# Operands of four operand sets made one stage early, kept in DRAM and fetched back, with four plain openings left out

## The chip, the cores and the metric

The kernel runs on one core of one Trainium2 chip. The metric is the time of one execution on the device in microseconds (us), lower is better; the profile is one execution taken by the hardware profiler.

## The reference

One encoder layer on 768 tokens (512 of the sample, 256 of the prompt) with 2048 channels, in float32. What matters here:

```python
h = _rms(x, norm_g) * (1 + scl) + shift            # adaLN: shift, scl, gate = silu(c) @ w_ada + b_ada
proj = h @ w_in                                    # 2048 -> 10240 = 80 blocks of 128 features
pool_u, pool_z, q, k, v, attn_z, g_pool, g_attn = split(proj)
pool_y = _pool_mixer(pool_u, pool_w, pool_scale) * silu(pool_z)
attn_y = _neighbourhood_attention(rms(q), rms(k), v, rpb) * silu(attn_z)
merged = sigmoid(g_pool) * (pool_y @ w_pool_up) + sigmoid(g_attn) * (attn_y @ w_attn_up)
return x + gate * (merged @ w_o)
```

## The kernel before

Everything lies with channels on the 128 partitions and the 768 tokens along the free dimension, in two halves of 384. A float32 value is split into two float32r pieces, high and low, and a product is made of three matmuls on them (high by high, weight high by operand low, weight low by operand high).

**Sets.** A set holds the operands of a quarter-size scheme with seven products: for four pairs `j` of channel tiles it has the tiles B11, T1, T2, B21, T3, T4, B22, 28 slots of 384 KB (high and low piece of 128x384). `T1` to `T4` are sums and differences of the raw quarters. The sets follow each other on TensorE: XA and XB (the two halves of the 2048 channels of h, both against all 80 blocks of `w_in`), XR (the mixer's result, against `w_pu`), XY (the attention's result, against `w_au`), MA and MB (the two halves of merged, against `w_o`).

**Jobs.** `pair_job` makes two blocks of 128 outputs out of seven products: 7 x 4 x 3 = 84 matmuls of 128x384. Jobs of one `pair_jobs` list overlap by two products, so that TensorE goes from job to job. `opening` makes the first two blocks of a set without the scheme, from the raw quarters B11, B12, B21, B22 in 96 matmuls (line L458), so that T1 to T4 may be made meanwhile. XB, XR, XY, MA and MB each begin with an opening.

**Order.** The program is written out by hand. `steps` runs TensorE's list; `prepare` keeps the weights' split (L329 on ScalarE, L330 and L353 on VectorE) three products ahead; a clock ticks once in two `j` (six matmuls, 14 ticks in a job), and all other work is put at a tick (`at`, `after`) or in the list `tasks`, which `pump` works off in order when there are slots. `build` puts a set's making into `tasks`: load raw tiles, split them with `Set.put` (a cast on ScalarE, L194, and a subtraction on VectorE, L198), make the differences (`differences`, L218 to L230). There are 45 slots. A set takes 28 of them, and so the next set is mostly made while the last job of the set in front gives its slots back, and in the opening. For XY the raw tiles are the attention's result, gated there with silu of `attn_z` (L1178, L1179).

Other work beside TensorE's: stage A also computes the modulation (`late_mm`); the first part of stage B the pooling mixer (`mix`, with sums on GpSimd, L712); the rest of stage B the attention of 8 head pairs, one every 42 ticks (three jobs) for the first `DENSE` = 5, then one every 56 (four jobs). Partial results go to `part_d` by transfers from GpSimd's queue, in stage B by accumulating ones. SP's queue loads the weights.

Of the kernel before, what the change touches and what calls it, by code (L numbers as in the profile page):

```python
# [16 lines left out]
P = 128  # L17
# [26 lines left out]
SLOTS = 45  # L44
# [7 lines left out]
def encoder_layer(ctx: ExitStack, tc: tile.TileContext, xT, cT, w_ada2, w_ada4, b_ada, norm_g, w_in, pool_w,  # L52
# [14 lines left out]
    heap = {"live": 0, "peak": 0, "spare": 6}  # L67
# [87 lines left out]
    pace = {"kind": "pair", "task": 0, "chore": 0}  # L155
    EVERY = {"plain": 1, "drop": 2, "pair": 3}

    def pump():
        now = clock["now"]
        if tasks and now >= pace["task"] and tasks[0][1]() and room() >= tasks[0][0] + heap["spare"]:  # L160
            pace["task"] = now + EVERY[pace["kind"]]
            tasks.pop(0)[2]()
# [24 lines left out]
    class Set:  # L187
        def __init__(self, name, pairs=PAIRS):
            self.name, self.pairs, self.ops, self.left = name, pairs, {}, 0
# [91 lines left out]

    hurry = {"on": False}
# [62 lines left out]
    def pair_job(stt, f1, f2, done, last=False):  # L345
# [24 lines left out]
        def p1():  # L370
            keep("p1")
            c["o1"], c["o2"] = output("o1"), output("o2")

        def p12():
            dve.tensor_tensor(c["o1"][:, 0, :], c["b"][:, :TH], c["p1"], op=ALU.add)

        def s3():
            keep("u3")
            dve.scalar_tensor_tensor(c["o2"][:, 1, :], c["u3"], -1.0, c["c"][:, :TH], op0=ALU.mult, op1=ALU.subtract)
# [169 lines left out]
    def attention(p, start, pace):  # L549
# [4 lines left out]
        def unit_(u):  # L554
# [110 lines left out]
            def out():  # L665
# [5 lines left out]
                if u == 5:  # L671
                    pool.dma_start(attn_d[p], o)
                    state["attended"] = p
                    free(2)

            stages = [(-6, fetch), (0, scores), (1, biased), (3, exps), (5, vtrans), (6, vsplit), (5, recip), (6, norm),
                      (9, ptrans), (10, psplit), (13, values), (14, out)]
            for d, fn in stages:
# [144 lines left out]
    def fourth(ps):  # L823
# [6 lines left out]
    pair_jobs([pair_job(XA, cut(w_in, a, 0), cut(w_in, b, 0), both(store_part(a), store_part(b)), n == len(jobsA) - 1)  # L830
               for n, (a, b) in enumerate(jobsA)])
# [30 lines left out]
    DENSE = 5  # L862
# [5 lines left out]
    for n, g in enumerate(GR):  # L868
        f = 2 * g
        zz = jobB(Z0 + f, Z0 + f + 1, z_done(f), z_done(f + 1))  # L870
        if n == 0:
            opening(XB, cut(w_in, U0 + f, 1), cut(w_in, U0 + f + 1, 1), u_done(f), u_done(f + 1))
            pair_jobs([zz])
        else:
            pair_jobs([jobB(U0 + f, U0 + f + 1, u_done(f), u_done(f + 1)), zz])
# [16 lines left out]
    pair_jobs([jobB(*j, n == len(jobs) - 2) for n, j in enumerate(jobs[1:])])  # L892


    def sig_load(f):
        state["sig", f] = slot("sig")
        sp.dma_start(flat(state["sig", f]), part_d[G0 + f])

    def sig_take(f):
        t = state["sig", f]  # L900
        act.activation(flat(t), flat(t), AF.Sigmoid)  # L901
        return t

    def pu_done(f):
        def go(i, t):
            sg = sig_take(f)
            dve.tensor_tensor(flat(t), flat(t), flat(sg), op=ALU.mult)
            pool.dma_start(mp_d[f], flat(t))
            free()
            release(t, 3)  # L910
            sig_load(f + 2)
        return go

    def au_done(f):
        def go(i, t):
            sg = sig_take(16 + f)
            dve.tensor_tensor(flat(t), flat(t), flat(sg), op=ALU.mult)  # L917
            free()
            if 16 + f + 2 < 32:
                sig_load(16 + f + 2)  # L920

            def add():
                pool.dma_start(flat(t), mp_d[f], accum_op=ALU.add)
                after(5, out)
# [5 lines left out]
            add()  # L930
# [37 lines left out]
    def eight(stt, w, s, done):  # L968
        opening(stt, cut(w, 0, s), cut(w, 1, s), done(0), done(1))
        pair_jobs([pair_job(stt, cut(w, 2 * i, s), cut(w, 2 * i + 1, s), both(done(2 * i), done(2 * i + 1)), i == 7)  # L970
                   for i in range(1, 8)])

    eight(XR, w_pu, 0, pu_done)
    eight(XY, w_au, 0, au_done)
# [321 lines left out]
```

## Time and profile before

| | |
|---|---|
| median of 3 runs | 2046.11 us (2041.65 to 2046.28) |
| the profiled execution | 2051.03 us, its span from first to last instruction 2049.3 us |
| mean granted TensorE clock | 0.973 of full speed |
| TensorE matmul busy | 1939.6 us, 95% |
| VectorE, ScalarE, GpSimd busy | 1330.4 (65%), 1023.1 (50%), 259.8 us (13%) |
| DMA | 331.92 MB, 162 GB/s over the span |

TensorE is the engine that is nearly always busy; the share tells the mean of stages with different limits, so the stretches where its matmuls come slower than elsewhere have to be looked for one by one. The stages in the trace: XA to about 690 us, XB with the mixer to 900 and with the attention to about 1470, XR to 1630, XY to 1780, MA to 1910, MB to the end.

### The profile page before, as it was taken

What the parts mean: (1) busy time and instruction counts of PE and PEld (TensorE: products, weight loads), DVE (VectorE), ACT (ScalarE), POOL (GpSimd) and SP (SyncE); (2) the same over time, 40 slices, a digit from 0 to 9 for tenths busy, and PEclk for the clock granted to TensorE, in tenths of its full rate; (3) what the DMA queues carried; (4) which work ended last, traced back from release to release, by engine and by line L of the source; (5) the groups of instructions that cost most, each with busy time, mean ns of one, the idle gap of its engine ahead of it and who ended that gap; (6) DMA issues with size and microseconds to landing.
All of it is one profiled execution on the core that took longest, in us unless ns stands there. A gap on an engine that the chain in (4) does not pass through costs nothing. (4 is left out here: it accounts for less than half of the span.)

```text
span 2049.3 us, 31584 instructions
## 1 busy us (share of the span) xinstructions
PE 1939.6 (95%) x11812; PEld 1832.7 (89%) x11812; DVE 1330.4 (65%) x2392; ACT 1023.1 (50%) x2207; POOL 259.8 (13%) x385
## 2 busy tenths in 40 slices
PE   3999999999999989999999999999989979999998
PEld 2889888898999979999998999999979968999997
DVE  5755555555667777866666667667667767776654
ACT  4433333333344444545656566565556555556553
POOL 0000000000000045410000010010100001112111
PEclk9999999999999999999999999999989989999999
DMA  9755555554343425554544344554556556867765
GB/s 355 248 197 188 190 191 191 201 192 157 117 150 138 162 57 143 135 132 106 119 106 122 93 110 122 109 121 123 132 164 216 214 158 180 243 180 191 211 172 144
DMA packets 100361, 331.92 MB, mean 162 GB/s; under 512 B 13168, under 2 KB 18288, under 8 KB 100208
## 3 DMA queue, kind: packets, MB, share of 16 engines
q1 hardware_dynamic: 68256, 217.35, 31.5%
q0 software_dynamic: 30944, 112.48, 23.8%
q8 instruction: 92, 1.51, 0.3%
q14 instruction: 61, 0.50, 0.1%
q10 hardware_dynamic: 1008, 0.09, 0.0%
HBM read 251.22 MB, written 78.64 MB: 161 GB/s over the span
## 5 line engine op out<-in xcount | busy, mean ns | idle before, releaser
L330 DVE TENSOR_TENSOR wlo<-wraw,whi 128x512 fp32r<-128x512 f32 (+1 forms) x357 | 247.2, 693 | 300.7 <-ACT whi L329 294.8
L330 DVE TENSOR_TENSOR wlo<-wsum,whi 128x512 fp32r<-128x512 f32 x420 | 292.7, 697 | 126.6 <-ACT whi L329 124.5
L440 PE MATMUL acc<-xbT,whi 128*128 128x384 f32 x1248 | 338.4, 352 | 10.6 <-ACT u L368 8.4
L329 ACT CAST whi<-wsum 128x512 fp32r<-128x512 f32 x420 | 260.4, 620 | 150.0 <-ACT whi L329 47.2
L440 PE MATMUL acc<-xaT,whi 128*128 128x384 f32 x1216 | 313.5, 338 | 1.1 <-ACT u L368 0.6
L329 ACT CAST whi<-wraw 128x512 fp32r<-128x512 f32 (+1 forms) x357 | 215.8, 605 | 97.4 <-PE acc L440 71.0
L368 ACT COPY u<-acc 128x384 f32<-128x384 f32 x210 | 100.5, 478 | 299.8 <-PE acc L440 299.8
L440 PE MATMUL acc<-xbB,whi 128*128 128x384 f32 x936 | 245.7, 343 | 0.5 <-DVE o L757 0.5
L440 PEld LDWEIGHTS acc<-xbT,whi 128*128 128x128 f32 x1248 | 226.2, 194 | 19.3 <-ACT u L368 10.6
L440 PE MATMUL acc<-xaB,whi 128*128 128x384 f32 x912 | 235.3, 338 | 0.0
L440 PEld LDWEIGHTS acc<-xaT,whi 128*128 128x128 f32 x1216 | 217.5, 188 | 16.2 <-issue 14.4
L440 PE MATMUL acc<-xbT,wlo 128*128 128x384 f32 x624 | 214.8, 344 | 0.0
L440 PE MATMUL acc<-xaT,wlo 128*128 128x384 f32 x608 | 203.7, 335 | 0.0
L440 PEld LDWEIGHTS acc<-xaB,whi 128*128 128x128 f32 x912 | 163.0, 188 | 11.9 <-issue 9.9
L440 PEld LDWEIGHTS acc<-xbB,whi 128*128 128x128 f32 x936 | 165.7, 189 | 6.0 <-issue 1.4
L440 PE MATMUL acc<-xbB,wlo 128*128 128x384 f32 x468 | 157.2, 336 | 0.0
L353 DVE TENSOR_TENSOR wsum<-wraw 128x512 f32<-128x512 f32 x210 | 145.1, 691 | 13.7 <-DMA wraw<-in_w_in_dram 13.6
L440 PE MATMUL acc<-xaB,wlo 128*128 128x384 f32 x456 | 152.8, 335 | 0.0
L353 DVE TENSOR_TENSOR wsum<-wsum,wraw 128x512 f32<-128x512 f32 x210 | 147.7, 703 | 0.2
L440 PEld LDWEIGHTS acc<-xbT,wlo 128*128 128x128 f32 x624 | 121.1, 194 | 0.0
L382 ACT ACTIVATE o<-acc 128x384 f32<-128x384 f32 x105 | 51.6, 492 | 125.3 <-PE acc L440 125.0
L440 PEld LDWEIGHTS acc<-xaT,wlo 128*128 128x128 f32 x608 | 114.1, 188 | 0.0
(251 smaller groups left out, 3435.4 us busy)
## 6 DMA issues: line engine op xcount, KB each, us to landing
wraw<-in_w_in_dram SPq DMA_DIRECT2D x160, 512.0 KB, 4.3
adaw<-in_w_ada_dram SPq DMA_DIRECT2D x96, 512.0 KB, 5.4
part_d<-o POOLq DMA_DIRECT2D x116, 384.0 KB, 2.9
wraw<-in_w_o_dram SPq DMA_DIRECT2D x32, 512.0 KB, 6.2
o<-part_d POOLq DMA_DIRECT2D x38, 384.0 KB, 4.8
sig<-part_d SPq DMA_DIRECT2D x32, 384.0 KB, 6.2
wraw<-in_w_pu_dram SPq DMA_DIRECT2D x16, 512.0 KB, 4.5
wraw<-in_w_au_dram SPq DMA_DIRECT2D x16, 512.0 KB, 5.0
```

The lines of the kernel that those rows point to most:

```text
L329: act.copy(hi[:, :n, :], raw)
L330: dve.tensor_tensor(lo[:, :n, :], raw, hi[:, :n, :].bitcast(F32), op=ALU.subtract)
L353: dve.tensor_tensor(t[:, :n, :], a, b, op=ALU.add)
L368: act.copy(t, c["a"][:, :TH])
L382: act.activation(c["o2"][:, 0, :], c["a"][:, :TH], AF.Copy, scale=-1.0)
L440: pe.matmul(out, w, m, start=s["first"] and j == 0 and k == 0, stop=j == n - 1 and k == 2, skip_group_check=True)
```

## The change

For XB, XR, XY and MB there is no opening: their first two blocks become an ordinary pair job, and their jobs stand in one list with those of the set in front, so that the last job of one set overlaps the first of the next. MA keeps its opening.

`store` makes a set's operands one stage early, out of a second list `back` that `pump` works off beside `tasks` (one entry in three ticks, at most `fly` tiles on their way): raw tiles are loaded, each operand is made with `Set.put` as before, written to DRAM by GpSimd's queue, and its slot is given back four ticks later. `recall` fetches the 28 operands into slots by GpSimd's queue, at most one a tick. XB is made in stage A, XR and XY during the attention, MB during MA. B12 is not made for these sets.

The attention's result is gated in the attention: `attn_z` loaded by SP, silu on ScalarE with a table load before and one after it, a product on VectorE. `DENSE` is 8, so every head pair takes 42 ticks. The sigmoids of the merge gates are taken six ticks after their load. In XB's making the modulation runs on ScalarE, where VectorE did it. 46 slots.

```diff
-SLOTS = 45
+SLOTS = 46
...
+    def store(st, load, ready=lambda j: True, make=None, last=None):
+        got = {}
+        def fetch(j):
+            got["a"], got["b"] = load(j)
+            got["t"] = clock["now"]
+        def save(op, j):
+            t = st.ops.pop((op, j))
+            st.saved[op, j] = d = dram.tile([P, 2, TH], F32R, name=f"{st.name}{op}{j}")
+            pool.dma_start(d, t)
+            def landed():
+                free()
+                heap["flying"] -= 1
+            after(4, landed)
...
+        def pair(j):
+            back.append((2, lambda: ready(j) and free_slot(), lambda: fetch(j)))
+            here = lambda: clock["now"] >= got["t"] + 6
...
+    def recall(st):
+        def load(op, j):
+            t = st.ops[op, j] = slot(f"{st.name}{op}", F32R)
+            pool.dma_start(t, st.saved[op, j])
+        for op in ORDER:
+            for j in range(st.pairs):
+                tasks.append((1, lambda op=op, j=j: (op, j) in st.saved, lambda op=op, j=j: load(op, j), 1))
...
+            def gate_on():
+                act.activation(flat(c["z"]), flat(c["z"]), AF.Silu)
+                act.preload_act_table_set(LNEXP)
...
-    DENSE = 5
+    DENSE = 8
...
-        if n == 0:
-            opening(XB, cut(w_in, U0 + f, 1), cut(w_in, U0 + f + 1, 1), u_done(f), u_done(f + 1))
-            pair_jobs([zz])
...
+    pair_jobs([*line, *eight(XR, w_pu, 0, pu_done), *eight(XY, w_au, 0, au_done)])
+    opening(MA, cut(w_o, 0, 0), cut(w_o, 1, 0), half_done(0), half_done(1))
+    pair_jobs([*eight(MA, w_o, 0, half_done, 1), *eight(MB, w_o, 1, y_done)])
...
-        build(XB, x_pair, lambda j: clock["now"] >= early, x_make, 0, 2)
+        recall(XB)
...
+        store(XR, lambda j: stored(pooled_d, 2 * j))
+        store(XY, lambda j: stored(attn_d, 2 * j), lambda j: state.get("gated", -1) >= 2 * j + 1)
...
+    store(MB, lambda j: stored(merged_d, 8 + 2 * j), lambda j: {8 + 2 * j, 9 + 2 * j} <= state.get("merged", set()))
+    run(16)
+    recall(MB)
```

TensorE's order before, where XR ends and XY begins (L440 are pair jobs, L458 the opening; `xrB`, `xyB` are tiles of the sets):

```order
L440 MATMUL acc<-xrB_15968,whi 128x384 x2
L440 MATMUL acc<-xrB_15968,wlo 128x384
L458 MATMUL acc<-xyB_16287,whi 128x384
L458 MATMUL acc<-xyB_16319,whi 128x384
L458 MATMUL acc<-xyB_16287,whi 128x384
L458 MATMUL acc<-xyB_16319,whi 128x384
L458 MATMUL acc<-xyB_16287,wlo 128x384
```

The same place after the change (L528 are pair jobs):

```order
L528 MATMUL acc<-xrT_16180,whi 128x384 x2
L528 MATMUL acc<-xrT_16180,wlo 128x384
L528 MATMUL acc<-xyB_16327,whi 128x384 x2
L528 MATMUL acc<-xyB_16327,wlo 128x384
L528 MATMUL acc<-xyB_16339,whi 128x384 x2
L528 MATMUL acc<-xyB_16339,wlo 128x384
L528 MATMUL acc<-xyB_16349,whi 128x384 x2
L528 MATMUL acc<-xyB_16349,wlo 128x384
L528 MATMUL acc<-xyB_16363,whi 128x384 x2
L528 MATMUL acc<-xyB_16363,wlo 128x384
L528 MATMUL acc<-xrT_16223,whi 128x384 x2
```

XY's first product now stands between two of XR's last job, where the opening stood behind all of them.

GpSimd's queue before, where MA ends and MB begins (L938 accumulates, L944 and L952 write results):

```order
L938 DMA o_19625<-in_xT_dram 128x768
L938 DMA o_19624<-in_xT_dram 128x768
L944 DMA half_d_258<-o_19625 128x768
L944 DMA half_d_257<-o_19624 128x768
L938 DMA po<-half_d_243 128x768
L938 DMA po<-half_d_244 128x768
```

The same place after the change, up to the last operand of MB (L363 is `recall`'s fetch, L1032 accumulates, L1038 writes):

```order
L363 DMA mbT_20274<-mbT_19215 128x768
L363 DMA mbT_20286<-mbT_19541 128x768
L1032 DMA o_20247<-in_xT_dram 128x768
L363 DMA mbT_20298<-mbT_19870 128x768
L363 DMA mbT_20312<-mbT_20219 128x768
L1032 DMA o_20216<-in_xT_dram 128x768
L363 DMA mbB_20324<-mbB_19052 128x768
L363 DMA mbB_20337<-mbB_19391 128x768
L1038 DMA half_d_258<-o_20247 128x768
L363 DMA mbB_20346<-mbB_19722 128x768
L363 DMA mbB_20358<-mbB_20054 128x768
L1038 DMA half_d_257<-o_20216 128x768
```

Fetches stand between the accumulating transfers and the writes of results, and the last ones stand behind the last of MA's accumulating transfers.

ScalarE's order after the change, in the attention, at a gate (L767, L768 the gate, L200 the cast of `Set.put`, L416 the weights' cast, L675 and L686 the softmax, L455 a copy of a finished sum):

```order
L686 ACTIVATE p<-p,rc 128x192 x2
L200 CAST xrT_10064<-in 128x384
L758 COPY o<-op 64x128 x2
L767 ACT_TABLE_LOAD
L767 ACTIVATE az<-az 128x768
L768 ACT_TABLE_LOAD
L416 CAST whi<-wraw 128x512
L455 COPY u_10111<-acc 128x384
```

The two table loads, the silu and the casts of the stored sets are new between the softmax, the weights' casts and the copies.

## Rows read from the trace of the kernel before

**Rows 1.** The profile page: span; busy time, share and instructions of TensorE.

```profile
span 2049.3 us, 31584 instructions
...
PE 1939.6 (95%) x11812; PEld 1832.7 (89%) x11812; DVE 1330.4 (65%) x2392; ACT 1023.1 (50%) x2207; POOL 259.8 (13%) x385
```

**Rows 2.** Busy time by stretch: start:end, length, engines (x instructions), clock, DMA share, GB/s.

```profile
540.00:690.00 150.00, 150.00 (x868) 150.00 (x867) 104.34 (x176) 65.75 (x127) 10.79 (x20) 1.00 0.39 136
690.00:790.00 100.00, 86.36 (x460) 83.04 (x459) 74.83 (x117) 43.76 (x88) 38.20 (x50) 0.94 0.44 116
790.00:900.00 110.00, 106.86 (x616) 105.29 (x615) 81.84 (x131) 55.78 (x107) 44.80 (x68) 0.99 0.54 138
1038.60:1103.50 64.90, 63.78 (x401) 58.67 (x401) 42.92 (x91) 39.07 (x110) 5.78 (x7) 0.97 0.46 106
...
1485.00:1560.00 75.00, 64.48 (x331) 61.95 (x330) 52.79 (x93) 42.98 (x79) 5.63 (x8) 0.91 0.54 172
1560.00:1620.00 60.00, 58.79 (x339) 58.38 (x338) 46.89 (x78) 33.56 (x61) 4.32 (x8) 1.00 0.61 215
1620.00:1720.00 100.00, 81.87 (x395) 77.06 (x394) 65.36 (x108) 55.44 (x95) 8.93 (x13) 0.86 0.54 170
1720.00:1780.00 60.00, 58.43 (x337) 58.11 (x336) 47.57 (x80) 32.93 (x62) 11.71 (x16) 1.00 0.89 241
1780.00:1835.00 55.00, 48.91 (x270) 47.95 (x269) 38.20 (x68) 31.37 (x64) 8.86 (x13) 0.97 0.70 190
...
1905.00:1955.00 50.00, 47.49 (x271) 46.53 (x270) 32.67 (x59) 29.11 (x59) 9.42 (x13) 1.00 0.67 174
1955.00:2010.00 55.00, 55.00 (x319) 55.00 (x319) 32.91 (x55) 29.47 (x56) 10.80 (x15) 1.00 0.74 188
```

**Rows 3.** TensorE's waits, 1620 to 1720 us: total us, times, longest us.

```profile
PE acc L440 <- ACT p L368: 6.8, 1, 6.8
PE acc L458 <- DVE xyB L198: 4.4, 2, 3.2
```

**Rows 4.** ScalarE in order of time at the same seam: start us, us, instruction.

```profile
1624.30 1.28 ACT L1178 ACT_TABLE_LOAD   x1
...
1626.97 1.28 ACT L901 ACT_TABLE_LOAD   x1
1628.26 0.85 ACT L901 ACTIVATE sig<-sig 128x768 f32<-128x768 f32 x1
```

**Rows 5.** Order of time at the seam of XA and XB.

```profile
738.69 2.07 POOL L712 TENSOR_TENSOR sum<-sum 128x785 f32<-128x785 f32 x1
738.95 2.36 DVE L353 TENSOR_TENSOR wsum<-wsum,wraw 128x512 f32<-128x512 f32 x1
...
746.04 0.50 PEld L440 LDWEIGHTS acc<-xbT,whi 128*128 128x128 f32 x2 [5.25 <-ACT u L368]
```

**Rows 6.** Busy time by stretch, matmuls of the pair jobs (L440) alone, in the attention.

```profile
972.50:1233.50 261.00, 203.19 (x1009) 175.77 (x1008) 0.97 0.47 110
1313.50:1391.50 78.00, 65.23 (x336) 58.82 (x336) 0.98 0.51 118
```

**Rows 7.** TensorE's waits in the attention, 910 to 1460 us: the longest group.

```profile
PE n L503 <- ACT sq L497: 2.1, 5, 0.4
```

**Rows 8.** Groups by line, ScalarE and VectorE: xcount | busy us, mean ns | idle before.

```profile
L194 ACT CAST xyT<-in 128x384 fp32r<-128x384 f32 x16 | 8.2, 512 | 18.8 <-DVE in L223 7.2 <-DVE in L218 6.2 <-DVE in L230 5.4
...
L1178 ACT ACTIVATE in<-in 128x768 f32<-128x768 f32 x8 | 6.5, 841 | 2.9 <-DMA in<-part_d 2.9
...
L198 DVE TENSOR_TENSOR xyT<-in,xyT 128x384 fp32r<-128x384 f32 x16 | 8.7, 552 | 1.2 <-ACT xyT L194 1.2
...
L1179 DVE TENSOR_TENSOR in<-in 128x768 f32<-128x768 f32 x8 | 7.5, 956 | 7.0 <-ACT in L1178 7.0
```

**Rows 9.** Transfers by line: count, KB each, median us from issue to landing.

```profile
part_d<-o POOLq DMA_DIRECT2D x116, 384.0 KB, 2.9
...
o<-part_d POOLq DMA_DIRECT2D x38, 384.0 KB, 4.8
```

More of the change, by code (lines that the diff above doesn't have):

```diff
@@ L280, in build, with put, done, free_slot @@
                 tasks.append((1, lambda: True, lambda j=j, n=n: diff(j, n)))
+    def store(st, load, ready=lambda j: True, make=None, last=None):
[11 more added lines that the diff above has]
+            after(4, landed)
+        def put(op, j, src, then=None):
+            heap["flying"] += 1
+            def done():
+                if then is not None:
+                    then()
+                save(op, j)
+            st.put(op, j, src, done)
+            mine = behind["of"]
+            after(2, lambda: flush() if behind and behind["of"] is mine else None)
+        def free_slot():
+            return heap["flying"] < heap["fly"]
+        def pair(j):
+            back.append((2, lambda: ready(j) and free_slot(), lambda: fetch(j)))
+            here = lambda: clock["now"] >= got["t"] + 6
+            if make is not None:
+                for k in "ab":
+                    back.append((0, here, lambda k=k: make(j, k, got[k])))
+            for op in ("B11", "B21", "B22"):
+                k, h = RAW[op]
+                back.append((1, lambda: here() and free_slot(), lambda op=op, k=k, h=h: put(op, j, got[k][:, h, :])))
+            def t1():
+                a = got["a"]
+                flush()
+                dve.tensor_tensor(a[:, 0, :], a[:, 0, :], a[:, 1, :], op=ALU.subtract)
+                put("T1", j, a[:, 0, :])
+            def t2():
+                a, b = got["a"], got["b"]
+                dve.tensor_tensor(a[:, 1, :], b[:, 1, :], a[:, 1, :], op=ALU.subtract)
+                dve.scalar_tensor_tensor(b[:, 1, :], a[:, 0, :], -1.0, b[:, 1, :], op0=ALU.mult, op1=ALU.subtract)
+                put("T2", j, b[:, 1, :])
+            def t3():
+                put("T3", j, got["a"][:, 1, :], free)
+            def t4():
+                b = got["b"]
+                dve.scalar_tensor_tensor(b[:, 0, :], b[:, 1, :], -1.0, b[:, 0, :], op0=ALU.mult, op1=ALU.subtract)
+                put("T4", j, b[:, 0, :], free)
+                if j == st.pairs - 1 and last is not None:
+                    after(6, last)
+            for fn in (t1, t2, t3, t4):
+                back.append((1, free_slot, fn))
+        for j in range(st.pairs):
+            pair(j)
@@ L282, in encoder_layer @@
+    def recall(st):
[3 more added lines that the diff above has]
+        for op in ORDER:
+            for j in range(st.pairs):
+                tasks.append((1, lambda op=op, j=j: (op, j) in st.saved, lambda op=op, j=j: load(op, j), 1))
     hurry = {"on": False}
@@ L915, in go @@
         def go(i, t):
[L916 to L924, printed above, removed]
+            gate_with(16 + f, t)
+            pool.dma_start(flat(t), mp_d[f], accum_op=ALU.add)
             def out():
@@ L929, in out @@
                 release(t, 3)
-            add()
+            after(5, out)
         return go
@@ L966, in y_done, with eight @@
         return go
[L968 to L974, printed above, removed]
-    eight(MA, w_o, 0, half_done)
-    eight(MB, w_o, 1, y_done)
+    def eight(stt, w, s, done, first=0):
+        return [pair_job(stt, cut(w, 2 * i, s), cut(w, 2 * i + 1, s), both(done(2 * i), done(2 * i + 1)), i == 7)
+                for i in range(first, 8)]
+    pair_jobs([*line, *eight(XR, w_pu, 0, pu_done), *eight(XY, w_au, 0, au_done)])
+    opening(MA, cut(w_o, 0, 0), cut(w_o, 1, 0), half_done(0), half_done(1))
+    pair_jobs([*eight(MA, w_o, 0, half_done, 1), *eight(MB, w_o, 1, y_done)])
     GROUPS = [(0, 2), (2, 2), (4, 2), (6, 2), (8, 4), (12, 4)]
@@ L1155, in encoder_layer @@
             pool.memset(state["u", i], 0.0)
-        run(16)
-        free()
-        run(8 * 14 + 4 * 4)
+        run(9 * 14 + 4 * 4 - 2)
     def pooled(j):
```

108 lines of the change are left out of this document (61 added, 47 removed).

## The prediction

> **What bounds the kernel now.** I read the page first: TensorE is busy 95% of a span of 2049.3 us [rows 1]. So a gain can only come from fewer matmuls or from the stretches where they come late, and the next view is busy time by stretch. From 540 to 690 us, where nothing but pair jobs runs, 868 matmuls take 150.00 us, 172.8 ns each [rows 2]; this is TensorE's full rate, at a granted clock of 1.00. For the other stretches that hold only 128x384 matmuls I take length less count times 172.8 ns as lost:
>
> - XA to XB: 690 to 790, 100 - 460 x 0.1728 = 20.5 us; 790 to 900, with the mixer, 3.6 us.
> - XB to XR: 1485 to 1560, 17.8 us, and 1.4 us up to 1620.
> - XR to XY: 1620 to 1720, 31.7 us, and 1.8 us up to 1780.
> - XY to MA: 1780 to 1835, 8.3 us.
> - MA to MB: 1905 to 1955, 3.2 us [rows 2].
>
> So the seams between sets cost 88 us. The waits tell why: in the worst one TensorE waits 6.8 us at once for a copy of a sum on ScalarE and 4.4 us for pieces of XY [rows 3]. ScalarE in order of time shows the copy's queue: it loads a table for the gate's silu, then one for the sigmoid, 1.28 us each, again and again [rows 4], with the casts of the set between. The granted clock falls with the idling, to 0.91 and 0.86 over these stretches [rows 2], so part of the lost time is matmuls at 1.2 instead of 2.4 GHz after a stall.
>
> The attention is different. TensorE hardly waits there: its longest group of waits in 550 us is 2.1 us [rows 7]. Its own small matmuls lie between those of the jobs.
>
> **What is taken away.** Four openings of 96 matmuls become jobs of 84: 48 x 0.1728 = 8.3 us.
>
> XR to XY: the gate's silu and table loads, the casts and the differences all leave the seam. TensorE's order shows XY's first product standing inside XR's last job. Of 33.5 us I take 29; at least 20, since other casts and the sigmoids stay, at most 33.5.
>
> XB to XR: of 19.2 us I take 17 (10 to 19.2) before what its fetches cost, below.
>
> XA to XB: not all of the 20.5 us belongs to the making of XB. A sum of weights on VectorE takes 2.36 us beside a mixer's sum of 2.07 us on GpSimd, where one of three quarters of its size takes 0.55 us alone [rows 8], and TensorE waits 5.25 us soon after [rows 5]; the mixer stays where it is. I take 14 (8 to 20.5).
>
> MA to MB: the 3.2 us. Together 8.3 + 29 + 17 + 14 + 3.2 = 71.5 us.
>
> **What is added.** *ScalarE and VectorE in the attention.* XR and XY bring 56 casts of 0.512 us, the gates 8 silus of 0.841 us [rows 8] and 16 table loads of 1.28 us [rows 4]: 28.7 + 6.7 + 20.5 = 56 us on ScalarE, 7.0 us in each head pair. VectorE gets 56 subtractions of 0.552 us, 32 differences of about the same and 8 products of 0.956 us [rows 8]: 31 + 18 + 8 = 57 us, 7.1 us a head pair. In a head pair of 64.9 us ScalarE is busy 39.07 and VectorE 42.92 us [rows 2], so they go from 60 and 66% to 71 and 77%. VectorE at 78% went with full TensorE from 1560 to 1620 (46.89 of 60 us, 1.4 us lost [rows 2]), so the load itself fits. What can reach TensorE is a burst: silu with its two loads holds ScalarE for 3.4 us, and the weights' casts, three products ahead, and the copies stand behind it. I take 6 us for the eight, from nothing up to all 56.
>
> The Trainium skill speaks against the gates: in "ScalarE: Activation LUTs", section "What ACT_TABLE_LOAD costs", each switch is 1.28 us of load and 1.38 us of drain, 2.66 us in all. By it a gate would hold ScalarE for 6.2 us and the sixteen loads cost 43 us, the sum 22 us more on that engine. The trace disagrees: the sigmoid begins 1.29 us after its load began [rows 4], with no drain between.
>
> *The denser attention.* Four head pairs at three jobs took 261.00 us with 1009 matmuls of the jobs, 65.25 us each; one at four jobs took 78.0 us [rows 6]. Moving a job out of three of them costs 3 x (65.25 + 84 x 0.1728 - 78.0) = 5.3 us.
>
> *The transfers.* 112 stores and 112 fetches of 384 KB (393,216 bytes). No such transfer is in the trace, so bounds. Where only plain transfers run, a DMA share of 0.39 moves 136 GB/s [rows 2], 349 GB/s for a full share: 1.13 us of all 16 engines for one. For the upper end, from 1955 to 2010 a share of 0.74 is 40.7 us; 319 matmuls are 3.8 jobs, each with two weights of 512 KB, two writes of 384 KB and two accumulating transfers. The plain ones take 20.0 us at 349 GB/s, which leaves 2.7 us for one that accumulates. A fetch moves each byte once, which is nearer to a plain transfer, so I take 1.13 us. Then 224 of them are 253 us of DMA in 2000, at a share now mostly of 0.4 to 0.7: enough on the whole, so what counts is where they crowd.
>
> - XA to XB: 11 fetches, 12 us of DMA, within 133 matmuls (23 us), the last used 18 us after its issue. Landing took 2.9 us for a write and 4.8 for an accumulating transfer [rows 9]. Hidden. Stage A's stores go beside jobs that leave half of the DMA.
> - XB to XR: within 277 matmuls (47.9 us) stand 30 stores and fetches, 6 accumulating transfers, 8 weights of 1.5 us and two gate loads: 34 + 16 + 12 + 2 = 64 us, 16.5 too many. The last fetch has 105 matmuls (18.1 us) to its use, less 2.9 us to land. I take 2 us (0 to 10).
> - XR to XY: 13 fetches in 144 matmuls; 26 us of DMA in 25, with 15 us to spare. Hidden.
> - MA to MB: here merged is finished late, and storing and fetching run in one piece. In 217 matmuls (37.5 us) stand 32 stores and fetches, 4 writes, 4 accumulating transfers and 6 weights: 36 x 1.13 + 4 x 2.7 + 6 x 1.5 = 60.5 us, 23 too many, and the last two fetches stand only four matmuls ahead of their use. So this seam is not closed; it now waits for the fetches instead of the splits. I take 18 us, since some of the queue is not needed by then (0 to 23).
>
> *MA's opening* stays, and its last tiles are split some 20 matmuls later against TensorE than before, with MB's loads beside them: 3 us (0 to 8). The sigmoids stand six ticks behind their load, 36 matmuls or 6.2 us, and transfers of that size landed in 2.9 to 4.8 us [rows 9]: nothing. If the queue is full, ScalarE waits for what a landing takes beyond 6.2 us, up to 32 times.
>
> Losses: 6 + 5.3 + 2 + 18 + 3 = 34.3 us.
>
> **The sum.** 71.5 - 34.3 = 37.2 us off the profiled execution's 2051.03 us gives 2013.8. That execution lies 4.9 us above the median of the runs, 2046.11, so 2009 us.
>
> **The rivals.**
> *Cheaper than that:* the gates and casts in the attention cost nothing and MB's fetches come in time, since its stores begin with the stage and the queue is drained ahead. For it speak the free ScalarE and the DMA share of 0.67 there [rows 2]; against it the 60 us of transfers counted above. 2009 - 6 - 18 = 1985 us.
> *Attention pays:* half of ScalarE's 56 us reaches TensorE, because ScalarE works in order and a silu also waits there for its load and a cast for its raw tile. Against it stands the full rate with VectorE at 78%. 2009 + 22 = 2031 us.
> *Slower:* a store or fetch costs what an accumulating transfer does, 2.7 us, because it is more than a copy. The tiles are float32r on both sides and go by GpSimd's queue. Then 32 at MB cost 1.57 us more each, 50 us; 30 at XR 47 us with 1 to spare; 13 at XY 20 us with 13 to spare: 50 + 46 + 7 = 103 us more, 2112 us. It decides from 37.2 / 103 of the way up, 1.7 us a transfer. Against it: an accumulating transfer reads two streams, a fetch one. The Trainium skill gives this rival a ground, in "DMA: Bandwidth & Descriptors", section "SWDGE vs HWDGE vs iDMA": a float32r source is read as float32, so one to float32r always casts. It gives no price for a cast, and no transfer in the trace of before shows one.
> That the change does not do what it says is excluded by the order shown above.
>
> **How the numbers follow.** The forecast (1990 to 2028) has 0.50, the cheap case 0.20, the paying attention 0.14, the dear transfers 0.12; 0.04 are for gains and waits that cancel. A measurement of this kernel tells 0.3%, 6 us, from no change. Faster: 0.50 + 0.20 and all but 0.01 of 0.14, 0.83; the same 0.04; slower 0.12 + 0.01 = 0.13. The range leaves out the dear transfers and a little at the low end: 1980 to 2043 us.
>
> **What would show it.** Right: stretches at the three first seams with 172 to 175 ns for a matmul and a clock of 1.00, no wait of L528 for xb, xr, xy; waits at MB's first job for fetched mb tiles, some 18 us in all; eight head pairs of 65 to 67 us. Wrong: fetches landing 10 us or more after issue at XR, or a DMA share near 1 over all of the attention (dear transfers); waits for ScalarE's copies in the attention (paying attention); MB's seam without waits (cheap).

## The result and the profile after

The changed kernel takes 2061.74 us (median of 4 runs, 2059.16 to 2064.7); the kernel before, timed beside it, 2043.88 us. The ratio is 1.0088, with a 95% interval of 1.0064 to 1.0111: slower by 0.9%, 18 us, where 37 us faster was forecast. Three of the experiments below had one execution each that was far slower than their others (2374, 3756 and 6425 us), which their times leave out. The profiled execution has a span of 2062.0 us, 12.7 us more than that of before [rows 1]. The page of the kernel after:

```profile
span 2062.0 us, 32106 instructions
...
PE 1934.4 (94%) x11764; PEld 1819.1 (88%) x11764; DVE 1339.9 (65%) x2400; ACT 1038.5 (50%) x2225; POOL 384.7 (19%) x609
```

The 48 matmuls of the openings are gone, and TensorE is busy 5 us less in a span that is 12.7 us longer. So it is idle 18 us more than before. To find them I marked in both traces the times at which VectorE adds up the same job's sums (to about 1 us, counted in 128x384 matmuls less the openings' extra ones) and compared the stages:

| stage | before | after | difference | forecast |
|---|---|---|---|---|
| start to the attention (seam XA to XB) | 898.8 | 879.9 | -18.9 | -16.1 |
| attention, seam XB to XR | 692.9 | 718.4 | +25.5 | -5.8 |
| rest of XR, seam XR to XY, XY | 205.1 | 170.9 | -34.2 | -31.1 |
| MA, seam MA to MB, MB | 252.4 | 292.8 | +40.4 | +15.7 |

Two stages keep the forecast, two are far off: the attention by 31 us, MA and MB by 25. First the seams, in busy time by stretch of the kernel after (columns as in [rows 2]):

```profile
600.00:720.00 120.00, 120.00 (x695) 120.00 (x694) 71.84 (x116) 48.55 (x92) 16.03 (x29) 1.00 0.46 159
...
1500.00:1660.00 160.00, 160.00 (x925) 160.00 (x925) 108.27 (x170) 79.27 (x140) 36.64 (x64) 1.00 0.87 292
1660.00:1765.00 105.00, 101.64 (x577) 99.45 (x577) 79.74 (x132) 54.62 (x102) 20.58 (x28) 1.00 0.85 234
...
1900.00:1960.00 60.00, 39.16 (x151) 32.62 (x150) 16.25 (x27) 15.09 (x29) 21.61 (x36) 0.69 0.94 279
```

The seams of XA to XB, XB to XR and XR to XY, which [rows 2] showed at clocks of 0.94, 0.91 and 0.86, now run without a break: 120 us with 695 matmuls and 160 us with 925 (both of the last two seams) are 172.7 and 173.0 ns each, at a clock of 1.00, even with the DMA engines busy 87%. The seam of MA to MB, of all, has become the worst stretch: 151 matmuls in 60 us, at a granted clock of 0.69.

In the attention, TensorE's longest group of waits is now the first row here, where the longest before had 2.1 us in all [rows 7]; the row behind it is the same wait before. Below them stand the pair jobs' matmuls (L528, before the change L440) from 909 to 1440 us, after and before, columns as in [rows 6]; before, the last three head pairs ran at the lower density, so part of the larger count is due to that:

```profile
PE vt L695 <- DVE pl L735: 29.1, 16, 3.7
PE vt L607 <- DVE pl L647: 1.3, 5, 0.3
```

```profile
909.00:1440.00 531.00, 392.89 (x1902) 337.32 (x1902) 0.94 0.58 150
909.00:1440.00 531.00, 428.14 (x2161) 377.02 (x2160) 0.97 0.48 113
```

Seven of these waits, one behind each gate but the last, are of 3.2 to 3.7 us. What they wait for is the p-split: the softmax's result p is transposed by TensorE into PSUM, ScalarE casts it to the high piece `ph`, and VectorE subtracts that to make the low piece `pl`. Around the first of them, ScalarE, then VectorE, then TensorE in order of time:

```profile
968.77 1.28 ACT L767 ACT_TABLE_LOAD   x1
970.07 0.84 ACT L767 ACTIVATE az<-az 128x768 f32<-128x768 f32 x1
970.93 1.28 ACT L768 ACT_TABLE_LOAD   x1
972.22 0.62 ACT L416 CAST whi<-wraw 128x512 fp32r<-128x512 f32 x1
...
973.76 0.63 ACT L730 CAST ph<-pt 128x256 fp32r<-128x256 f32 x2
```

```profile
972.87 0.69 DVE L417 TENSOR_TENSOR wlo<-wraw,whi 128x512 fp32r<-128x512 f32 x1 [5.10 <-ACT whi L416]
973.48 0.95 DVE L772 TENSOR_TENSOR o<-o,az 128x768 f32<-128x768 f32 x1
...
977.53 0.74 DVE L735 TENSOR_TENSOR pl<-pt,ph 128x256 fp32r<-128x256 f32 x2
```

```profile
978.42 0.44 PE L695 MATMUL vt<-ident,o 128*128 128x128 f32 x1 [3.69 <-DVE pl L735]
```

The reader is to see one chain. The gate of the head pair in front holds ScalarE from 968.77 to 972.21: load, silu, load. The weight's cast stands behind it, VectorE stands idle 5.10 us for that cast, and the whole of what has gathered (the gate's product, the biased scores, a maximum, weights) goes ahead of `pl`. Until that has read the transposed p, its PSUM tile is taken, and the next unit's transpose of V, which has the same one, holds up TensorE with all jobs behind it.

At MB's start, TensorE's waits from 1900 to 1960 us, its order of time, the stretch with the lowest clock (columns as in [rows 2]), and GpSimd's queue:

```profile
PE acc L528 <- DMA mbT<-mbT: 14.3, 5, 3.9
PE acc L528 <- DMA mbB<-mbB: 6.4, 6, 2.1
```

```profile
1903.17 0.51 PE L528 MATMUL acc<-mbT,whi 128*128 128x384 f32 x2
...
1907.71 0.63 PE L528 MATMUL acc<-mbT,whi 128*128 128x384 f32 x2 [3.85 <-DMA mbT<-mbT]
...
1913.32 1.01 PE L528 MATMUL acc<-mbT,whi 128*128 128x384 f32 x2
...
1918.53 1.01 PE L528 MATMUL acc<-mbT,whi 128*128 128x384 f32 x2 [3.88 <-DMA mbT<-mbT]
...
1928.93 1.01 PE L528 MATMUL acc<-mbB,whi 128*128 128x384 f32 x2 [0.55 <-DMA mbB<-mbB]
...
1939.57 0.51 PE L528 MATMUL acc<-mbB,whi 128*128 128x384 f32 x2
```

```profile
1910.00:1940.00 30.00, 17.35 (x48) 13.03 (x49) 4.52 (x8) 2.61 (x5) 12.02 (x21) 0.52 1.05 331
```

```profile
1893.72 0.54 POOL L299 DMA_DIRECT2D mbT<-mbT  x1
1904.27 0.54 POOL L363 DMA_DIRECT2D mbT<-mbT  x1 [10.01 <-issue]
...
1907.82 1.23 POOL L363 DMA_DIRECT2D mbT<-mbT  x1
1917.82 0.55 POOL L363 DMA_DIRECT2D mbT<-mbT  x1 [8.77 <-DMA mbT<-mbT]
```

The waits for fetched tiles are there as forecast, 20.7 us. But between them two matmuls take 1.01 us instead of 0.51: the granted clock of this stretch is 0.52, the level of 1.2 GHz. And the queue shows why the tiles come in lumps: the fetch at 1904.27 (L363) is that of the tile whose store was issued at 1893.72 (L299). It waits 10.01 us in the queue for that store to land, with all later fetches, outputs and accumulating transfers behind it; the wait of 8.77 us at 1917.82 is the same for another tile.

### The profile page after: what moved, and what is told of

Same layout as the page of the kernel before. It is cut to its first block, busy times and chain, and to the rows that moved or that the text cites. A ratio compares the mean times of both kernels' runs of the same rounds, so it can differ in the third digit from the quotient of the medians.

```text
span 2062.0 us, 32106 instructions
## 1 busy us (share of the span) xinstructions
PE 1934.4 (94%) x11764; PEld 1819.1 (88%) x11764; DVE 1339.9 (65%) x2400; ACT 1038.5 (50%) x2225; POOL 384.7 (19%) x609
## 3 DMA queue, kind: packets, MB, share of 16 engines
q0 software_dynamic: 63200, 200.57, 35.6%
## 4 chain that ended last, share of the span: by engine, by line
PE 73%; DVE 7%; DMA 6%; ACT 6%; issue 5%; POOL 2%; SPq 0%; POOLq 0%; ACTq 0%; DVEq 0%
PE acc L528 63%; PE adaacc L565 2%; DVE wlo L417 2%; PE op L750 2%; DMA o<-in_xT_dram 2%; PE acc L546 1%; ACT whi L416 1%; DMA adaw<-in_w_ada_dram 1%; PE n L591 1%; DMA mbB<-mbB 1%; PE s L656 1%; DVE wsum L440 1%; DMA in<-merged_d 1%; PE pt L717 1%; PE yk L627 1%
## 5 line engine op out<-in xcount | busy, mean ns | idle before, releaser
L417 DVE TENSOR_TENSOR wlo<-wsum,whi 128x512 fp32r<-128x512 f32 x436 | 312.3, 717 | 142.3 <-ACT whi L416 137.7
L528 PE MATMUL acc<-xbT,whi 128*128 128x384 f32 x1280 | 348.8, 354 | 7.7 <-ACT u L455 7.7
L416 ACT CAST whi<-wsum 128x512 fp32r<-128x512 f32 x436 | 270.4, 620 | 144.8 <-ACT whi L416 53.9
L528 PE MATMUL acc<-xaT,whi 128*128 128x384 f32 x1216 | 313.6, 338 | 1.0 <-DVE xaT L204 0.5
L416 ACT CAST whi<-wraw 128x512 fp32r<-128x512 f32 (+1 forms) x353 | 213.4, 605 | 89.8 <-PE acc L528 76.6
L528 PE MATMUL acc<-xbB,whi 128*128 128x384 f32 x960 | 254.0, 345 | 1.7 <-DVE o L861 1.7
L528 PEld LDWEIGHTS acc<-xbT,whi 128*128 128x128 f32 x1280 | 231.3, 195 | 18.4 <-ACT u L455 12.0
L455 ACT COPY u<-acc 128x384 f32<-128x384 f32 x218 | 104.1, 477 | 275.1 <-PE acc L528 274.7
L528 PE MATMUL acc<-xaB,whi 128*128 128x384 f32 x912 | 235.2, 338 | 0.0
L528 PEld LDWEIGHTS acc<-xaT,whi 128*128 128x128 f32 x1216 | 217.4, 188 | 16.3 <-issue 14.0
L528 PE MATMUL acc<-xbT,wlo 128*128 128x384 f32 x640 | 220.8, 345 | 0.2 <-DVE wlo L417 0.2
L528 PE MATMUL acc<-xaT,wlo 128*128 128x384 f32 x608 | 203.7, 335 | 0.0
L528 PEld LDWEIGHTS acc<-xbB,whi 128*128 128x128 f32 x960 | 171.4, 190 | 8.8 <-issue 2.7
L528 PEld LDWEIGHTS acc<-xaB,whi 128*128 128x128 f32 x912 | 163.0, 188 | 11.9 <-issue 9.9
L528 PE MATMUL acc<-xbB,wlo 128*128 128x384 f32 x480 | 161.9, 337 | 0.0
L528 PE MATMUL acc<-xaB,wlo 128*128 128x384 f32 x456 | 152.8, 335 | 0.0
L440 DVE TENSOR_TENSOR wsum<-wraw 128x512 f32<-128x512 f32 x218 | 150.9, 692 | 0.1
L440 DVE TENSOR_TENSOR wsum<-wsum,wraw 128x512 f32<-128x512 f32 x218 | 149.8, 687 | 0.3
L528 PEld LDWEIGHTS acc<-xbT,wlo 128*128 128x128 f32 x640 | 124.4, 194 | 0.5 <-DVE wlo L417 0.5
L874 POOL DMA_DIRECT2D part_d<-o x76 | 41.2, 542 | 446.0 <-ACT o L470 368.9
L528 PEld LDWEIGHTS acc<-xaT,wlo 128*128 128x128 f32 x608 | 114.2, 188 | 0.0
```

The costliest lines, as they stand in the source:

```text
L416: act.copy(hi[:, :n, :], raw)
L417: dve.tensor_tensor(lo[:, :n, :], raw, hi[:, :n, :].bitcast(F32), op=ALU.subtract)
L440: dve.tensor_tensor(t[:, :n, :], a, b, op=ALU.add)
L455: act.copy(t, c["a"][:, :TH])
L528: pe.matmul(out, w, m, start=s["first"] and j == 0 and k == 0, stop=j == n - 1 and k == 2, skip_group_check=True)
L874: pool.dma_start(part_d[f], flat(t))
```

## The experiments

My theory: the attention's loss is the gate's burst on ScalarE, by its place ahead of a p-split; MB's loss is its transfers, the clock behind the waits included. The rivals: the stores' casts and differences, the denser attention, or ScalarE's load as a whole in the attention; MA's own work at the end.

**Without the silu.**

```diff
             def gate_on():
-                act.activation(flat(c["z"]), flat(c["z"]), AF.Silu)
-                act.preload_act_table_set(LNEXP)
+                pass
```

> Leaves out the silu of the attention's gate with its two table loads (the gate then multiplies by the bare projection); stores, fetches and the denser attention stay. If the gate's 3.4 us burst on ScalarE makes the attention's loss: no wait of 3.7 us for the p pieces, a head pair at 65.5 to 67 us instead of 71.5, 2015 to 2025 us. If the stores' casts and differences or the density make it: the waits stay, a head pair at 70 us or more, 2050 to 2060 us.

2029.82 us, ratio 0.9942 (0.9922 to 0.9961); this kernel leaves out the gate's function, so it shows a cost and is no repair. The waits for `pl` and the jobs' matmuls in the same 531 us:

```profile
PE vt L695 <- DVE pl L735: 9.3, 15, 1.2
```

```profile
909.00:1440.00 531.00, 413.11 (x2061) 359.22 (x2062) 0.96 0.61 160
```

159 matmuls more in the same time. At the mark behind the seam of XB to XR it is 31.3 us ahead of the change: this is the whole cost of the burst. The forecast had 6 us of it, so of the 31 us by which the stage missed the forecast 25 are the burst. The stores and the density were still there, and with all else they are left the other 6 us; the waits for `pl` that remain, 9.3 us against 1.3 before the change, are of that size. (The time is some 5 us above the range that I had expected.)

**The gate four ticks later.**

```diff
-                stages += [(8, gate_load), (14, gate_on), (15, gated)]
+                stages += [(8, gate_load), (18, gate_on), (19, gated)]
```

> The same gate, four ticks later in the head pair (silu at tick 18 of unit 5, product at 19), just behind a p-split instead of just ahead of one. If the place of the burst decides: the 3.7 us waits go or shrink below 1 us, a head pair at 66 to 68 us, 2020 to 2035 us, with all the table loads kept. If ScalarE's load as a whole decides: no gain, 2055 to 2062 us.

2042.34 us, ratio 0.9998 (0.9981 to 1.0015), 19 us under the change with every table load kept:

```profile
PE vt L695 <- DVE pl L735: 7.4, 16, 1.0
PE acc L528 <- ACT u L455: 4.8, 3, 1.8
```

Of the 31 us more than half hang on the place. The rest does not go, and the time stays 7 us above the expected range: by the second row the block of 3.4 us now meets a copy of a sum (1.8 us).

**V's transposes off the shared PSUM tile.**

```diff
-                vt = ps_aux.tile([P, 512], F32, tag="pt", name="vt")
+                vt = ps_aux.tile([P, 512], F32, tag="vo", name="vt")
...
-            stages = [(-6, fetch), (0, scores), (1, biased), (3, exps), (5, vtrans), (6, vsplit), (5, recip), (6, norm),
+            stages = [(-6, fetch), (0, scores), (1, biased), (3, exps), (3, vtrans), (4, vsplit), (5, recip), (6, norm),
```

> The gate stays as in the change; V's transposes take the PSUM tile of the output products instead of the one that they share with the transposed p, two ticks earlier, with three instead of two buffers for V's pieces. If the late p-split reaches TensorE through that shared PSUM tile: the 3.7 us waits go, waits for weights of 1 to 2 us are left, 2025 to 2040 us. If ScalarE's burst holds up the weights' casts as much: waits of 3 us for those come in their place, 2052 us or more.

2074.79 us, ratio 1.0143 (1.011 to 1.0175): slower than the change by 13 us. That is in the second theory's range, but not by its mechanism, waits for weights. (V's pieces also have three buffers instead of two here.) The waits for `pl` are gone, but:

```profile
PE op L750 <- DVE vl L710: 20.6, 16, 3.0
PE op L750 <- DVE vs L710: 8.3, 7, 1.2
```

Now V's split is late behind the same burst (it stands behind `pl` on VectorE, at 983.30 us), and the output products, with which the transposes share a PSUM tile here, wait for it. So the shared tile was only where the delay showed. What is late is VectorE; moving the buffer moves the wait.

**Exp instead of silu, bunched and spread** (both with MB built, the next but one). The gate's factor is made with the loaded table as exp(-ln(1 + exp(-z))):

```diff
+                act.activation(flat(c["e"]), flat(c["z"]), AF.Exp, scale=-1.0)
...
+                act.activation(flat(c["e"]), flat(c["e"]), AF.Ln, bias=ones[:, 0:1])
...
+                act.activation(flat(c["e"]), flat(c["e"]), AF.Exp, scale=-1.0)
...
+                dve.tensor_tensor(flat(c["z"]), flat(c["z"]), flat(c["e"]), op=ALU.mult)
...
+ bunched:      stages += [(4, gate_load), (11, gate_on), (13, gate_ln), (14, gate_inv), (15, gate_mul), (16, gated)]
+ spread:       stages += [(4, gate_load), (11, gate_on), (18, gate_ln), (25, gate_inv), (26, gate_mul), (32, gated)]
```

> MB built as before the change, and the attention's gate made from the functions of the loaded table, exp, ln and exp again, in three separate steps with one product more on VectorE, so without table loads. If the burst with its two loads makes the attention's loss: no wait of 3 us there, a head pair of 66 to 68 us, and the sum of both repairs, 1988 to 1998 us. If three passes of 0.84 us cost as much as one with two loads: 2015 us or more.

2007.99 us, ratio 0.9812 (0.9792 to 0.9832), a miss: 16 us under `mb_built`, but 10 above the range. No table is loaded, yet the waits for `pl` are still 24.1 us, the longest 3.3. VectorE in order of time has both products of the gate, 0.95 us each, ahead of the split:

```profile
973.16 0.95 DVE L777 TENSOR_TENSOR az<-az,ez 128x768 f32<-128x768 f32 x1
...
976.00 0.95 DVE L782 TENSOR_TENSOR o<-o,az 128x768 f32<-128x768 f32 x1
...
978.08 0.74 DVE L735 TENSOR_TENSOR pl<-pt,ph 128x256 fp32r<-128x256 f32 x2
```

> As exp_mb, with the three passes of the gate seven ticks apart, each just behind a p-split, and its two products apart too. If it is the bunching ahead of a p-split that costs: no wait above 1.2 us in the attention, a head pair of 66.5 to 67.5 us, 1988 to 1998 us. If ScalarE's and VectorE's load as a whole: 2005 us or more.

1991.22 us, ratio 0.9746 (0.9721 to 0.9771), the fastest kernel here. The same three passes and two products, each behind a p-split; the waits, and the jobs' matmuls as above:

```profile
PE vt L695 <- DVE pl L735: 5.2, 13, 0.9
```

```profile
909.00:1440.00 531.00, 418.39 (x2092) 364.26 (x2091) 0.97 0.62 160
```

The same work in another order is 17 us faster (14 by the two ratios), so the bunching is the cause, not the load. `gate_no_silu` less the 37.4 us that MB built gains would be 1992.4: spread out, the whole gate costs nothing that shows, if the two gains add up (to 3 us they do, see `later_mb`).

**The density put back.**

```diff
-    DENSE = 8
+    DENSE = 5
```

> Only the density is put back: the last three head pairs get four jobs and a pace of 8. If the gate's place decides, the silu of these pairs falls in the gap between two head pairs, three of the eight waits go with their clock and 5.3 us of density come back: 2038 to 2046 us. If the density alone decides: 5 us, 2057 us. If the stores decide: 2057 to 2062 us.

2064.49 us, ratio 1.0116 (1.0094 to 1.0139): no gain, where 16 to 24 us were expected. The attention did become 22 us shorter, its last three pairs without the long wait; this holds their waits and the density together, and no run parts the two. But the next seam gave it all back; TensorE's waits from 1500 to 1535 us and the stretch:

```profile
PE acc L528 <- DMA xrT<-xrT: 9.7, 9, 3.6
```

```profile
1505.00:1535.00 30.00, 18.01 (x68) 12.93 (x67) 9.80 (x18) 5.68 (x11) 12.56 (x22) 0.76 1.13 383
```

The program asks for XR's fetches when the attention is over. So the jobs that the denser attention moves behind itself are the time in which they land. Without them 68 matmuls take 30 us.

**MB built as before.**

```diff
-    pair_jobs([*eight(MA, w_o, 0, half_done, 1), *eight(MB, w_o, 1, y_done)])
+    pair_jobs(eight(MA, w_o, 0, half_done, 1))
+    opening(MB, cut(w_o, 0, 1), cut(w_o, 1, 1), y_done(0), y_done(1))
+    pair_jobs(eight(MB, w_o, 1, y_done, 1))
...
-    store(MB, lambda j: stored(merged_d, 8 + 2 * j), lambda j: {8 + 2 * j, 9 + 2 * j} <= state.get("merged", set()))
...
-    recall(MB)
...
+    build(MB, lambda j: stored(merged_d, 8 + 2 * j), lambda j: {8 + 2 * j, 9 + 2 * j} <= state.get("merged", set()), whole=2)
```

> MB alone is made as before the change, in SBUF with a plain opening; the rest of the change stays. If MB's 64 transfers crowd the queue and cost the 21 us of waits and the clock behind them: the stretch from the first MA job to the end shrinks by 30 to 38 us, 2024 to 2032 us. If the loss there comes from MA's own transfers and the sigmoids: 10 us or less, 2050 us or more.

2024.35 us, ratio 0.9916 (0.9892 to 0.994): 37 us under the change, as expected. From XY's end to the end it takes 250 us, against 293. The opening's extra matmuls cost 2.1 us; storing MB cost twenty times that.

**Four tiles kept; stores earlier; both; fetches asked for later.** A tile that is wanted as soon as it is stored stays in SBUF (`mb_keep`); MB's steps follow every two ticks instead of three (`mb_fast`); or, with these earlier stores, a fetch is asked for twelve ticks after its store at the earliest (`fast_wait`).

```diff
 mb_keep, in save():
+            if st.want and st.want[0] == (op, j):
+                st.want.pop(0)
+                heap["flying"] -= 1
+                return
...
 mb_fast, in pump(), and ahead of MB's store:
-            pace["back"] = now + 3
+            pace["back"] = now + heap["gap"]
...
+    heap["gap"] = 2
...
 fast_wait, in recall():
-                tasks.append((1, lambda op=op, j=j: (op, j) in st.saved, lambda op=op, j=j: load(op, j), 1))
+                tasks.append((1, lambda op=op, j=j: (op, j) in st.saved and clock["now"] >= st.at[op, j] + (12 if st is MB else 0), lambda op=op, j=j: load(op, j), 1))
```

> A tile of MB that is asked for as soon as it is stored stays in SBUF: four of the 28 are neither stored nor fetched, and four of the six fetches that stand in GpSimd's queue right behind their own store fall away (7.4, 5.4, 7.1 and 10.0 us of waiting there; the one of 8.8 us at the seam stays). If this blocked queue makes MB's loss: the waits at MB's first jobs fall from 21 to under 8 us, 2030 to 2045 us. If the amount of transfers in the seam does: only 8 of 56 transfers go, some 8 us, 2050 to 2056 us.

> MB's casts, differences and stores follow each other every two ticks instead of three, so that the last store stands 176 matmuls earlier and the last fetch 81; all 28 stores and 28 fetches stay. If the lateness of the stores (the crowd in the last 37 us before MB) makes the loss: the waits at MB's first jobs go to under 5 us, 2022 to 2035 us. If 56 transfers are too many for the whole stretch wherever they stand: the waits move into MA's jobs, 2050 us or more.

> Both repairs of MB's transfers together, the gate as in the change. If they take away the same waits: as the earlier stores alone, 2020 to 2035 us; MB built in SBUF gave 2024 us. If kept tiles matter beside them: 8 us less than the earlier stores alone.

> As mb_fast, all 28 stores and 28 fetches, but a fetch is asked for twelve ticks after its store at the earliest, so that none stands in GpSimd's queue for its own store to land. If the blocked queue costs the time that the kept tiles gave back: as with kept tiles and early stores, 2040 to 2046 us. If the number of transfers costs it: as mb_fast, 2055 to 2060 us.

They took 2045.46 (ratio 0.9996, 0.9984 to 1.0009), 2058.13 (1.0057, 1.0042 to 1.0072), 2043.94 (0.9988, 0.9978 to 0.9998) and 2046.33 us (1.0009, 0.9996 to 1.0022). Keeping four tiles takes 8 of 56 transfers away and gains 16 us, to the edge of the expected range; the waits for fetched tiles at MB's first jobs fall from 20.7 to 8.8 us. Earlier stores alone gain 4, a miss: fetches still stood behind their own stores, and MA's jobs lost 8 us more, as the rival had it. `fast_wait` has all 56 transfers and gains 12 us on `mb_fast` (10 by the ratios), at the edge of the range expected; kept tiles with the same early stores (`keep_fast`) gain 14, short of the range expected. So the order in GpSimd's queue is worth 10 to 12 us by itself. The waits for fetched tiles in `fast_wait`, from 1900 to 1960 us:

```profile
PE acc L529 <- DMA mbT<-mbT: 5.2, 3, 3.2
```

By marks, in us:

| | MA's jobs | seam and MB's first jobs |
|---|---|---|
| change | 134.1 | 114.2 |
| mb_keep | 131.4 | 100.5 |
| mb_fast | 142.4 | 98.0 |
| fast_wait | 142.1 | 88.0 |
| mb_built | 126.5 | 80.8 |

**What is left in MA.** `wait_later` is `fast_wait` with MB's making begun 20 ticks later (its fetches may begin 4 later); `fast_wait_no_x` and its control `mb_built_no_x` take the 16 transfers that add x out of MA.

```diff
 wait_later, ahead of MB's store and behind it:
+    run(20)
...
-    run(16)
...
 the other two, in half_done():
-            gated_out(f, t, xT[:, f, :], out)
+            gated_out(f, t, None, out)
```

> As fast_wait, but MB's making begins 20 ticks later, behind MA's opening, so that its casts no longer stand ahead of MA's last ones on ScalarE; the last fetches then crowd again, 24 in some 130 matmuls. If MB's casts at MA's opening cost MA's jobs their time: from XY's end through MA's jobs 126 to 131 us instead of 142, as with MB built (126.5); the seam behind it, 88 us in fast_wait, then rises to 95 to 105 by the crowd, 2040 to 2050 us in all. If MA's jobs pay for the transfers wherever they are: 140 us or more in MA, 2046 us or more.

> As fast_wait, and MA's outputs leave out the addition of x, that is its 16 accumulating transfers; all 56 transfers of MB and all its casts stay. If the DMA's load in MA and at the seam makes what is left of MB's loss (24 us from XY's end on, against MB built): 12 to 24 us less than fast_wait, 2022 to 2034 us. If MB's casts and differences on ScalarE and VectorE make it: 2042 us or more.

> The control: MB built, and MA's outputs without the addition of x. With a DMA share of 0.75 in MA its transfers are hidden, so under either theory the 2024 us of mb_built, within 4 us.

`wait_later`: 2055.65 us (1.006, 1.0043 to 1.0077), 138.7 us in MA's jobs and 97.1 at the seam; a miss, since in MA only 3.4 us of the 15.6 between `fast_wait` and `mb_built` came back, and the crowd at the seam cost 9. The second: 2036.77 us (0.9964, 0.9948 to 0.998), between the two ranges expected; the control 2024.1 (0.9905, 0.9881 to 0.993), as expected. Stretches of `fast_wait`, then of `fast_wait_no_x`:

```profile
1770.00:1912.00 142.00, 126.20 (x689) 124.32 (x688) 98.45 (x176) 78.75 (x159) 47.88 (x79) 0.95 0.96 291
1912.00:2000.00 88.00, 82.80 (x459) 81.15 (x458) 47.09 (x77) 43.10 (x82) 21.94 (x33) 0.96 0.83 219
```

```profile
1770.00:1912.00 142.00, 125.85 (x688) 123.98 (x687) 98.34 (x176) 79.38 (x160) 39.13 (x72) 0.95 0.81 275
1912.00:2000.00 88.00, 88.00 (x509) 88.00 (x508) 51.97 (x86) 47.40 (x90) 17.18 (x25) 1.00 0.75 210
```

In MA the DMA share falls from 0.96 to 0.81 and TensorE does the same 688 matmuls; so MA's loss is not the DMA's load. At the seam the 16 transfers do count: without them, full rate. Whether by their load on the DMA or by their place in GpSimd's queue is not parted: in `fast_wait` that queue waits 22.2 us for them to land before it writes results, and without them it does not. In MA, TensorE's waits from 1775 to 1885 us are all for copies on ScalarE, 11.0 us in the kernel after against 4.0 in `mb_built`. A sign of what makes the copies late is in ScalarE's order in `wait_later`:

```profile
1816.04 0.51 ACT L200 CAST mbT<-in 128x384 fp32r<-128x384 f32 x1 [2.29 <-DVE in L341]
1816.46 0.47 ACT L456 COPY u<-acc 128x384 f32<-128x384 f32 x1
```

A cast of MB waits 2.29 us for VectorE's difference, and the copy of a sum, for which TensorE waits 3.16 us at 1816.98, stands behind it. Such a pair at each of several places was read, not tested; and `wait_later`, which moves MB's casts, gave little back. So that the casts are the cause in MA is not shown.

**The repairs together.**

> MB built and the silu gate four ticks later, V's transposes where the change has them. If the loss in the attention and that at MB are separate: the two gains, 18 and 37 us, add up to 2004 to 2010 us. If one hides part of the other: 2015 us or more.

> MB built, the gate by silu and table loads but four ticks later, and V's transposes off the shared PSUM tile. If these two repairs add up: no waits above 2 us in the attention, a head pair of 66.5 to 68 us, 1990 to 2002 us. If they take away the same waits: as MB built with the later gate alone, 2005 to 2010 us.

`later_mb` takes 2002.11 us (0.9792, 0.9776 to 0.9807): 60 us under the change and 2 below the expected range, where the two repairs alone sum to 57, so the two losses are separate. `all_mb`, which also moves V's transposes, takes 2035.54 (0.9958, 0.9943 to 0.9974), 33 more and a miss of both ranges: the output products wait for V's split again, since the moved gate now stands on ScalarE right ahead of V's cast, and VectorE waits 3.57 us for that cast at 981.20 us.

## Why the prediction was wrong

**The seams** were right: three of them run at full rate, no wait for xb, xr or xy tiles is left that matters, and the two stages that hold the first and the third gained 53.1 us where 47.2 were forecast. In part this was luck: the terms took 2.9 us for a transfer to land, and the fetches themselves took far longer. Fetches of XB from 530 to 700 us and of XR from 1470 to 1521 us, columns as in [rows 9]:

```profile
xbT<-xbT POOLq DMA_DIRECT2D x16, 384.0 KB, 9.5
xrT<-xrT POOLq DMA_DIRECT2D x16, 384.0 KB, 11.3
```

Landings of 10 us or more at XR were to be the sign of dear transfers. They came, but the transfers were not dear (below), only crowded, at a DMA share of 1.09 to 1.13 (1470 to 1535 us), and the lead of the fetches was enough. (The 16.5 us too many that I counted at XR are 16.1 by the terms given.)

**Openings** were right as counted (48 matmuls fewer).

**The burst in the attention is the first step that failed.** I named the mechanism, a silu with two loads that holds ScalarE for 3.4 us with casts behind it, and took 6 us for eight of them. It cost 31 us, by `gate_no_silu`, five times the term. The mistake was to judge by load ("VectorE at 78% went with full TensorE") and by ScalarE alone. A burst there is passed on in order: VectorE idles 5.10 us for a cast and then has its own backlog, and a PSUM tile with one buffer hands the delay to TensorE. The rival *attention pays* gave 22 us more than the forecast for this place, because ScalarE works in order; that is what happened, with 25 more, though by the gate's burst and its place and not by half of all of ScalarE's added work.

**MB's fetches are the second.** I counted 60.5 us of transfers in 37.5 and took 18 us, with 23 as the upper bound; the waits came to 20.7 us. That the count met them is in part luck: with the same 56 transfers in another order they are 5.2 us (`fast_wait`), so the amount alone does not make them. The term took the wait as the whole price, and its bound knew only the DMA's capacity. At 1.2 GHz the matmuls between the waits take twice their time: against full rate (457 matmuls, 79.0 us) the seam lost 35. And I said nothing of what a fetch does in GpSimd's queue: fetches there stood 5.4 to 10.0 us for their own stores. Against MB built, storing MB cost 42.5 us; the terms for all from MA on gave 15.7 against the kernel before, and it was 40.4. From the experiments: some 18 us are the order and lateness of stores and fetches (`fast_wait` takes them back). 15.6 us are lost in MA's jobs (7.6 at the change's own pace, where more falls to the seam), with the cause open. 8.8 us at the seam go with the transfers of x, by their load or their place in the queue.

**MA**, 3 us (0 to 8), measured 7.6 against MB built, at its upper end. It reaches TensorE through late copies on ScalarE; that they stand behind casts which wait for VectorE was read at one place and is not shown as the cause.

**The denser attention**, 5.3 us, is measured by no run alone, and it is not a price that can be saved: `dense5` shows that it buys the time in which XR's fetches land, and with it the 2 us of that term.

**Transfers' price** was right. The software queue's row of the page, of the kernel before and then of after:

```profile
q0 software_dynamic: 30944, 112.48, 23.8%
```

```profile
q0 software_dynamic: 63200, 200.57, 35.6%
```

23.8% of 2049.3 us are 487.7 us, 35.6% of 2062.0 are 734.1 us: 246 us for 224 transfers, 1.10 us each, against 1.13 taken. The rival of dear transfers (2.7 us) falls.

Together: by the table the attention fell short of its forecast by 31 us (25 of them the burst) and MA with MB by 25, and the seams gained 6 more: 50 us, which is the way from 37 us faster to 13 us slower in the profiled executions. The range ended at 2043 because no case that it took in had the attention and MB dear at once.

## What to carry to other kernels

Work that is moved under another stage is to be placed, not only weighed: look for the instruction on the critical chain that will stand behind it on each in-order engine, and cut it into pieces that fit between two such instructions; the gate cost 32 us as one block with its table loads, some 16 as three bunched passes, and next to nothing with these spread out. Never ask for a fetch in a queue while the store that it needs is still under way, and do not store what is wanted back at once. A seam that already loses only 3 us (MA to MB, [rows 2]) has little to give; moving this one cost 40.

## What the chip showed that I had not expected

Where waits of 2 to 4 us follow each other, the clock makes two fifths of the price: of the 35 us that MB's seam lost 20.7 are waits, and the rest falls where the matmuls run at the lower level. From 1908 to 1939 us two matmuls take up to 1.01 us instead of 0.51, though the last wait of over 3 us ended at 1918.53.

ScalarE goes on at once after a table load: the silu starts at 970.07, 1.30 us after its load began, and the cast 1.29 us after the load back began. The Trainium skill, in "ScalarE: Activation LUTs", section "What ACT_TABLE_LOAD costs", adds a drain of 1.38 us to each switch; here, as before the change, the rows show none, and the loss came without it.

A landing takes longer where transfers crowd. A line of the kernel after, columns as in [rows 9]:

```profile
part_d<-o POOLq DMA_DIRECT2D x116, 384.0 KB, 4.3
```

The same write took 2.9 us before, at 162 GB/s over the span; now it is 204 GB/s. So a landing of 10 us tells of the crowd and not of the price of a transfer. All queues together move 383 GB/s at a DMA share of 1.13 (1505 to 1535 us in `dense5`), and the float32r tiles cost no more than the estimate for plain ones (1.10 against 1.13 us). The Trainium skill says in "DMA: Bandwidth & Descriptors", section "SWDGE vs HWDGE vs iDMA", that a float32r source to a float32r target casts; if these did, the cast shows no price.
